# A quarter of the tokens sent ahead through every stage with unsplit weights, and more tokens moved from dense experts to gathered rows

## The chip, the core and the metric

The program runs on one core of one Trainium2 chip. The metric is the device time of one execution in microseconds (us). The engines are TensorE (PE, matmuls), VectorE (DVE), ScalarE (ACT), GpSimd (POOL) and the queues that issue transfers (SP's above all).

## What is computed

The reference is one residual block on x of 512 tokens by 2048 channels, all in float32:

```python
h  = rms_norm(x)
q, k, v, forget, pool_in, gates = split(h @ W_in)       # 8 heads x 128; pool 1024; two gates x 2048
yA = forgetting_attention(q, k, v, log_sigmoid(forget)) # causal, logits + sum of log f
yB = multiscale_pool(pool_in)                           # trailing means of 2, 4, 8, 16 tokens
x  = x + (sig(gA) * (yA @ W_A) + sig(gB) * (yB @ W_B)) @ W_out
xn = rms_norm(x)
# per token and head: 16 of 16384 experts by two lists of 128 keys (top 16 of each, then of their sums)
a   = u[idx] . xn                    # one number for each of 8 x 16 experts
x   = x + sum(gelu(a) * softmax_gate * v[idx])
```

An expert is one row of u and one row of v (2048 numbers each). The attention of a token needs the keys and values of all earlier tokens.

## The kernel before

**Weights as a stream.** Every weight tile is [128, 2048] float32, 1 MB. `plan` lists the tiles in the order of use; `ensure_load` (L112, the transfer is L116) brings them on SP's queue into `wraw` (three buffers). `ensure_split` makes two parts that TensorE takes at its fast rate: ScalarE casts `whi` (L131), then VectorE, for 28 tiles GpSimd, subtracts `wlo` (L133); two buffers each. `next_w` hands out tile n and has tile n+1 split at that place of the program. Activations are split in the same manner. `mm3` (L165 to L167) is three matmuls for each pair of blocks: high by high, high by low, low by high. A tile is 16 blocks, 48 matmuls.

**Stages.** All 512 tokens go together as columns through 64 tiles of input projections (with pooling, and attention head by head), 16 of the branch projection (`wbr`), 16 of the output projection (`wo`) and 16 of the query (`wqu`), with the top-k lists. Then the experts: the first 384 tokens are dense. For them all 16384 experts are computed: 128 tiles `uT` (128 experts each) give `a`, gelu, times a gate matrix that is zero except at the chosen experts, and 128 tiles `vd` bring the result back to channels. The first 64 u tiles run before any v tile and their results are spilled to `a_d`; meanwhile the gate matrix is built from comparisons (`o`, L801, L802, L804), small full-precision matmuls (L789) and copies to `stg`, and stored in `g_d`. Then come 192 tiles of u and v in turn.

**Gathered rows.** For the last 128 tokens the chosen rows are gathered: 128 indirect transfers of u (128 tokens x 2048, L832), each followed on VectorE by a multiply with a sum (L817), then 128 of v with a multiply and add (L823). Two buffers `row`; they are spread evenly over the 256 expert tiles.

**Who sets the order.** Each engine takes its instructions in the order of the program. Between two weight tiles the program calls `run_gens`, which lets every Python generator in `gens` (attention, norms, top-k, gates, the products `h_make` with the gates) issue its next piece. In an expert tile of before the rows come after that:

```python
        hi, lo = next_w()      # cast whi, subtract wlo of the next tile
        run_gens()
        rows_use()
        ps = acc_bank()
        mm3(ps[:, :ND], wterms(hi, lo, xnh, xnl))
```

`h_make` (L886) multiplies a block `at` (or a spilled one, `sp`) with its gates on VectorE, casts it on ScalarE (`h5h`) and subtracts on VectorE (`h5l`). A tick below is the work between two weight tiles.

Of the kernel before, what the change touches and what calls it, by code (L numbers as in the profile page):

```python
# [29 lines left out]
ND = 384  # L30
NDB = ND // P
# [8 lines left out]
LEAD = 14  # L40
QS = 2


@with_exitstack
def block_kernel(ctx, tc, a):
# [5 lines left out]
    wsp = ctx.enter_context(tc.tile_pool(name="wsp", bufs=2))  # L51
    psm = ctx.enter_context(tc.tile_pool(name="psm", bufs=4, space=bass.MemoryType.PSUM))
    psx = ctx.enter_context(tc.tile_pool(name="psx", bufs=4, space=bass.MemoryType.PSUM))
# [10 lines left out]
    z_d = dram.tile([2 * KD, P, S], F32, name="z_d")  # L64
    ap_d = dram.tile([4, P, 4, S], F32, name="ap_d")
    x2_d = dram.tile([4, P, 4, S], F32, name="x2_d")
    x2t_d = dram.tile([P, D], F32, name="x2t_d")
    a_d = dram.tile([LAG, P, IG, ND], F32, name="a_d")
    c_d = dram.tile([H, S], F32, name="c_d")
    g_d = dram.tile([NC, P, P, TC], F32, name="g_d")  # L70

    # weight stream: every tile is [128, 2048], read once, split into two float32r parts
    plan = []

    def flat(ap):
        return ap.rearrange("p j t -> p (j t)")

    order1 = [("g", 0), ("g", 1), ("pin", 0), ("pin", 1), ("pg", 0)] + [("pin", i) for i in range(2, 8)]
    gi = 2
    for h in range(H):  # L80
        order1 += [("q", h), ("k", h), ("v", h)] + [("g", gi + i) for i in range(3)]
        gi += 3
    order1 += [("g", i) for i in range(gi, 2 * KD)]
    src1 = dict(g="wgl", pin="wpin", q="wq", k="wk", v="wv")
    for kind, i in order1:
        plan.append((a["wpg"] if kind == "pg" else a[src1[kind]][i],
                     None if kind == "pg" else "dve"))
    for i in range(KD):
        plan.append((a["wbr"][i], "dve"))
        if i == 0:  # L90
            for c in (2, 3, 0):
                plan.append((flat(ap_d[c]), None))
    for i in range(KD):
        plan.append((a["wo"][i], "dve"))
    for i in range(KD):
        plan.append((a["wqu"][i], "pool"))
    seq = [("u", g) for g in range(LAG)]
    for g in range(LAG, NIG):
        seq += [("u", g), ("v", g)]
        if g - LAG < LAG:  # L100
            seq.append(("v", g - LAG))
    for n, (kind, g) in enumerate(seq):
        for i in range(4):
            eng = "pool" if n < 3 else "dve"
            if kind == "u":
                plan.append((a["uT"][g * IG + i], eng))
            else:
                plan.append((a["vd"][4 * g + i], eng))
# [11 lines left out]
    def ensure_split(n):  # L120
        while st["split"] <= min(n, len(plan) - 1):
            i = st["split"]
            st["split"] += 1
            eng = plan[i][1]
            if eng is None:
                n += 1
                continue
            ensure_load(i)
            raw = raws.pop(i)
            hi = wsp.tile([P, D], F32R, name="whi")  # L130
            nc.scalar.copy(hi, raw)  # L131
            lo = wsp.tile([P, D], F32R, name="wlo")
            (nc.gpsimd if eng == "pool" else nc.vector).tensor_tensor(  # L133
                lo, raw, hi.bitcast(F32), op=OP.subtract)
            parts[i] = (hi, lo)

    def next_w(ahead=1):
        n = st["use"]
        st["use"] += 1
        ensure_split(n)  # L140
        if ahead:
            ensure_load(n + 2)
            ensure_split(n + ahead)
        return parts.pop(n)

    def next_raw():
        n = st["use"]
        st["use"] += 1
        ensure_load(n)
        st["split"] = max(st["split"], n + 1)  # L150
        return raws.pop(n).rearrange("p (j t) -> p j t", j=4)
# [20 lines left out]

    def split(pool, src, shape, tag, **kw):
# [11 lines left out]

    g1 = const.tile([P, KD], F32, name="g1")
    nc.scalar.dma_start(g1, a["g1"])

    # stage 1: input projections, pooling branch, forgetting attention
    es_h, ph = lpool("ph")  # L190
    hh = ph.tile([P, KD, S], F32R, name="hh")
    hl = ph.tile([P, KD, S], F32R, name="hl")
    es_0, p0 = rpool("p0")
    xr = []
    ensure_load(0)
    for c in range(4):
        t = p0.tile([P, 4, S], F32, name="x%d" % c)
        nc.sync.dma_start(t.rearrange("p j t -> p (j t)"), a["xT"][c])
        xr.append(t)
    ensure_load(2)  # L200
    ensure_split(0)

    for c in range(4):
        for j in range(4):
            k = 4 * c + j
            nc.scalar.activation(hh[:, k, :], xr[c][:, j, :], AF.Copy, scale=g1[:, k:k + 1])  # L206
            nc.vector.scalar_tensor_tensor(hl[:, k, :], xr[c][:, j, :], g1[:, k:k + 1],  # L207
                                           hh[:, k, :].bitcast(F32), op0=OP.mult, op1=OP.subtract)
    ensure_split(1)
    first_z = [acc_bank()]  # L210
    hi, lo = next_w(0)
    mm3(first_z[0], wterms(hi, lo, hh, hl))
    ensure_load(2)
    jp = p0.tile([P, P], I32, name="jp")
# [9 lines left out]
    nc.vector.memset(epsc, EPS)  # L224
    rcnt = const.tile([P, 16], F32, name="rcnt")
# [3 lines left out]
    nc.scalar.dma_start(g2, a["g2"])  # L229
    psc = const.tile([P, 8], F32, name="psc")  # L230
    nc.scalar.dma_start(psc, a["psc"])
    qg = const.tile([P, 1], F32, name="qg")
    nc.scalar.dma_start(qg, a["qg"])
    nc.vector.tensor_scalar(qg, qg, float(np.float32(P ** -0.5)), None, op0=OP.mult)
    kg = const.tile([P, 1], F32, name="kg")
    nc.scalar.dma_start(kg, a["kg"])
    fb = const.tile([H, 1], F32, name="fb")
    nc.scalar.dma_start(fb, a["fb"])

    ssqx = const.tile([P, S + NTB], F32, name="ssq")  # L240
    ssq = ssqx[:, :S]
    sqs = []
    for c in range(4):
        t = p0.tile([P, 4, S], F32, name="s%d" % c, bufs=1) if c < 2 else xr[c]
        nc.scalar.activation(t, xr[c], AF.Square)
        sqs.append(t)
        if c == 1:
            nc.vector.tensor_tensor(sqs[0], sqs[0], sqs[1], op=OP.add)
    hi, lo = next_w()
    nc.vector.tensor_tensor(sqs[2], sqs[2], sqs[3], op=OP.add)  # L250
    nc.vector.tensor_tensor(sqs[0], sqs[0], sqs[2], op=OP.add)
    nc.vector.tensor_tensor(sqs[0][:, 0:2], sqs[0][:, 0:2], sqs[0][:, 2:4], op=OP.add)
    nc.vector.tensor_tensor(ssq, sqs[0][:, 0], sqs[0][:, 1], op=OP.add)
    es_0.close()
    first_z.append(acc_bank())
    mm3(first_z[1], wterms(hi, lo, hh, hl))
    es_1, p1 = rpool("p1")
    rstd = p1.tile([P, S], F32, name="rstd")
    jq = p1.tile([P, P], I32, name="jq")
    nc.gpsimd.iota(jq, pattern=[[1, P]], base=0, channel_multiplier=-1)  # L260
    onesr = p1.tile([P, P], F32R, name="onesr")
    nc.vector.tensor_copy(onesr, ones)
    mask = p1.tile([P, P], F32, name="mask")
    nc.vector.tensor_scalar(mask, jq, 0.0, 1.0e30, op0=OP.is_gt, op1=OP.mult)

    def rsqrt_of(out, tmp, ms, dst=None):
        nc.scalar.activation(out, ms, AF.Ln, bias=epsc[:, 0:1], scale=1.0)
        nc.scalar.activation(out, out, AF.Exp, scale=-0.5)
        nc.vector.tensor_tensor(tmp, out, out, op=OP.mult)
        nc.vector.scalar_tensor_tensor(tmp, ms, epsc[:, 0:1], tmp, op0=OP.add, op1=OP.mult)  # L270
        nc.vector.tensor_scalar(tmp, tmp, -0.5, 1.5, op0=OP.mult, op1=OP.add)
        nc.vector.tensor_tensor(out if dst is None else dst, out, tmp, op=OP.mult)

    def mean_bcast(sq, n, ms):
        ps = bank()
        nc.tensor.matmul(ps, lhsT=ones, rhs=sq, start=True, stop=True)
        nc.scalar.activation(ms, ps, AF.Copy, scale=1.0 / n)

    def input_norm():
        mean_bcast(ssq, D, ssq)  # L280
        t = p1.tile([P, S], F32, name="sc", bufs=4)
        rsqrt_of(rstd, t, ssq)

    def scaled(ps, tag, bufs):
        t = p1.tile([P, S], F32, name=tag, bufs=bufs)
        nc.vector.tensor_tensor(t, ps, rstd, op=OP.mult)
        return t

    def gate(i, ps):
        z = scaled(ps, "zg", 2)  # L290
        if i == 2 * KD - 1:
            nc.sync.dma_start(z_d[i], z)
        else:
            gens.append(gate_out(i, z))

    def gate_out(i, z):
        nc.sync.dma_start(z_d[i], z)
        yield

    mixes = {}  # L300

    def pool_in(i, ps):
        g, kc = divmod(i, 2)
        w = WINDOWS[g]
        raw = scaled(ps, "qkv", 3)
        cur, step = raw, 1
        while step < w:
            nxt = p1.tile([P, S], F32, name="sc", bufs=4)
# [9 lines left out]
        if kc == 1:  # L318
            gens.append(pool_group(g))
# [125 lines left out]
    for n, (kind, i) in enumerate(order1):  # L445
        if n < 2:
            continue
# [588 lines left out]
```

## Time and profile before

| | us |
|---|---|
| median of 3 runs | 3636.14 (3634.03 to 3636.44) |
| span of the profiled execution | 3634.7 |
| TensorE busy | 3555.3 |
| VectorE busy | 2435.5 |
| ScalarE busy | 1383.7 |
| GpSimd busy | 458.9 |
| projections with attention, about | 9 to 794 |
| branch, output, query stages, about | 794 to 1343 |
| first 64 u tiles and gate matrix, about | 1343 to 2066 |
| u and v tiles, about | 2066 to 3631 |

The profiled execution's span is 1.4 us under the median, so the sums below are made against the span and carried over with that difference. A busy share is an average over stages with different limits; the stages are read from windows.

### The profile page before, as it was taken

The numbers are of one execution on the slowest core, as the hardware profiler recorded it, in microseconds if no ns is written. First come the engines' busy times: TensorE is split into PE (matmuls) and PEld (weight loads), VectorE is DVE, ScalarE is ACT, GpSimd is POOL, SyncE is SP. The second block draws the span as 40 slices with busy tenths as digits, with TensorE's granted clock in tenths as the row PEclk, the third lists the DMA queues.
The fourth block names the chain that finished last, engine by engine and source line by source line (L and its number), as shares of the span: only waits on it lengthen the run. The fifth ranks groups of instructions, "written<-read, shape, count | busy, mean of one in ns | idle before, by whom it ended". The sixth has DMA issues, their size and how long they took to land.

```text
span 3634.7 us, 46381 instructions
## 1 busy us (share of the span) xinstructions
PE 3555.3 (98%) x19033; PEld 3315.7 (91%) x19033; DVE 2435.5 (67%) x3348; ACT 1383.7 (38%) x1735; POOL 458.9 (13%) x330
## 2 busy tenths in 40 slices
PE   8999999999999997699999999999999999999999
PEld 6788888878888877699999999999999999999999
DVE  5555445534432899466666677888888877778886
ACT  4343334323322431488887322222222222222222
POOL 0000000000001653111101111111111111111110
PEclk9999999999999998799999999999999999999999
DMA  4223332244444332378888978888788888788885
GB/s 186 87 103 109 110 113 99 102 169 146 154 145 137 116 113 100 120 284 300 279 281 291 342 279 293 292 288 292 277 302 281 289 290 282 272 288 293 288 291 203
DMA packets 187124, 789.56 MB, mean 217 GB/s; under 512 B 16264, under 2 KB 86920, under 8 KB 103840
## 3 DMA queue, kind: packets, MB, share of 16 engines
q1 hardware_dynamic: 132992, 469.80, 37.5%
q0 software_dynamic: 37040, 269.57, 20.6%
q10 hardware_dynamic: 16880, 47.23, 3.6%
q8 instruction: 149, 2.44, 0.3%
q14 instruction: 63, 0.52, 0.0%
HBM read 726.75 MB, written 59.79 MB: 216 GB/s over the span
## 4 chain that ended last, share of the span: by engine, by line
PE 92%; DVE 5%; issue 2%; POOL 1%; ACT 0%; DMA 0%; SPq 0%; POOLq 0%; ACTq 0%
PE psm L167 24%; PE psm L165 24%; PE psm L166 24%; PE psx L167 5%; PE psx L166 5%; PE psx L165 5%; PE psx L789 2%; DVE cf L675 1%; POOL wlo L133 0%; DVE pi L692 0%; DVE eqm L695 0%; DVE ix L622 0%; DVE s L617 0%; DVE ix L615 0%; DVE sel L703 0%
## 5 line engine op out<-in xcount | busy, mean ns | idle before, releaser
L133 DVE TENSOR_TENSOR wlo<-wraw,whi 128x2048 fp32r<-128x2048 f32 x340 | 781.7, 2299 | 533.3 <-ACT whi L131 533.1
L131 ACT CAST whi<-wraw 128x2048 fp32r<-128x2048 f32 x368 | 702.8, 1910 | 686.9 <-PE psm L166 360.6
L165 PE MATMUL psm<-xnh,whi 128*128 128x384 f32 x2048 | 696.4, 340 | 44.7 <-ACT whi L131 44.7
L167 PE MATMUL psm<-xnh,wlo 128*128 128x384 f32 x2048 | 692.0, 338 | 11.9 <-POOL wlo L133 11.9
L166 PE MATMUL psm<-xnl,whi 128*128 128x384 f32 x2048 | 691.5, 338 | 0.0
L165 PEld LDWEIGHTS psm<-xnh,whi 128*128 128x128 f32 x2048 | 387.8, 189 | 45.7 <-ACT whi L131 45.5
L165 PE MATMUL psm<-hh,whi 128*128 128x512 f32 x1024 | 403.8, 394 | 11.9 <-ACT hh L206 9.3
L167 PE MATMUL psm<-hh,wlo 128*128 128x512 f32 x1024 | 401.6, 392 | 1.3 <-DVE wlo L133 1.3
L166 PE MATMUL psm<-hl,whi 128*128 128x512 f32 x1024 | 401.0, 392 | 0.6 <-DVE hl L207 0.6
L167 PEld LDWEIGHTS psm<-xnh,wlo 128*128 128x128 f32 x2048 | 387.4, 189 | 13.2 <-POOL wlo L133 13.2
L166 PEld LDWEIGHTS psm<-xnl,whi 128*128 128x128 f32 x2048 | 387.8, 189 | 0.0
L167 PE MATMUL psx<-h5h,wlo 128*128 128x384 f32 x1024 | 342.3, 334 | 0.0
L165 PE MATMUL psx<-h5h,whi 128*128 128x384 f32 x1024 | 342.3, 334 | 0.0
L166 PE MATMUL psx<-h5l,whi 128*128 128x384 f32 x1024 | 342.2, 334 | 0.0
L167 PE MATMUL psm<-h5h,wlo 128*128 128x384 f32 x1024 | 342.1, 334 | 0.0
L166 PE MATMUL psm<-h5l,whi 128*128 128x384 f32 x1024 | 342.1, 334 | 0.0
L165 PE MATMUL psm<-h5h,whi 128*128 128x384 f32 x1024 | 342.1, 334 | 0.0
L823 DVE SCALAR_TENSOR_TENSOR tok<-row,gact,tok 128x2048 f32<-128x2048 f32 x128 | 300.3, 2346 | 2.8 <-DMA row<-v,gidx 2.6
L817 DVE SCALAR_TENSOR_TENSOR row<-row,tok 128x2048 f32<-128x2048 f32 x128 | 292.1, 2285 | 0.1
L832 POOL DMA_INDIRECT row<-u,gidx x128 | 136.3, 1065 | 960.0 <-DVE row L817 949.9
L832 POOL DMA_INDIRECT row<-v,gidx x128 | 137.5, 1074 | 845.8 <-DVE tok L823 800.7
L165 PEld LDWEIGHTS psm<-hh,whi 128*128 128x128 f32 x1024 | 193.6, 189 | 52.3 <-ACT hh L206 9.3
(263 smaller groups left out, 5392.0 us busy)
## 6 DMA issues: line engine op xcount, KB each, us to landing
wraw<-uT SPq DMA_DIRECT2D x128, 1024.0 KB, 5.3
wraw<-vd SPq DMA_DIRECT2D x128, 1024.0 KB, 4.9
wraw<-wgl SPq DMA_DIRECT2D x32, 1024.0 KB, 5.0
g_d<-stg ACTq DMA_DIRECT2D x12, 2048.0 KB, 8.9
gt<-g_d SPq DMA_DIRECT2D x32, 768.0 KB, 7.6
wraw<-wbr SPq DMA_DIRECT2D x16, 1024.0 KB, 7.7
wraw<-wo SPq DMA_DIRECT2D x16, 1024.0 KB, 4.9
wraw<-wqu SPq DMA_DIRECT2D x16, 1024.0 KB, 5.1
```

The source lines that it names most:

```text
L131: nc.scalar.copy(hi, raw)
L133: (nc.gpsimd if eng == "pool" else nc.vector).tensor_tensor(lo, raw, hi.bitcast(F32), op=OP.subtract)
L165: nc.tensor.matmul(ps, lhsT=wh, rhs=xh, start=first and i == 0, stop=False)
L166: nc.tensor.matmul(ps, lhsT=wh, rhs=xl, start=False, stop=False)
L167: nc.tensor.matmul(ps, lhsT=wl, rhs=xh, start=False, stop=last and i == n - 1)
L675: nc.vector.tensor_tensor(cf.rearrange("p (a b) -> p a b", a=TK), prev[0][:, :, None].to_broadcast([P, TK, TK]), prev[1][:, None, :].to_br ...
L789: nc.tensor.matmul(pg[:, j * P:(j + 1) * P], lhsT=o1[:, j, :], rhs=o2[:, j, :], start=True, stop=True)
L817: nc.vector.scalar_tensor_tensor(r, r, 1.0, tok, op0=OP.mult, op1=OP.mult, accum_out=gact[:, j:j + 1])
L823: nc.vector.scalar_tensor_tensor(tok, r, gact[:, j:j + 1], tok, op0=OP.mult, op1=OP.add)
L832: nc.gpsimd.indirect_dma_start(out=r, out_offset=None, in_=a["u"] if n < HK else a["v"], in_offset=bass.IndirectOffsetOnAxis(ap=gidx[:, j: ...
```

## The change

The first 128 tokens (`NA`) go alone through projections, attention, branch, output, query and top-k, with the weight tiles as they are: `mm1` takes them unsplit in full precision, 16 matmuls of 128 columns a tile. Their 112 weight tiles are loaded for them a first time. Then the other 384 tokens (`NB`) go through the same stages as before, with split weights loaded again; keys and values of the first 128 are kept in DRAM. Under these stages the 256 rows of the first 128 tokens are gathered, from the projections on, at a rate of rows a tile that `RATE_B1`, `RATE_B2` and `RATE_LAG` set. Of the 384 tokens the last 64 (`NG`) are gathered too, two lists' halves to a slot (`GQ`), 128 more rows, so 384 rows in all, and 320 (`ND`) are dense. All `wlo` are on VectorE. The top-k of two of the three later token blocks moves from the query stage into the first 64 u tiles, beside the gate matrix. v tiles are cut differently (8 experts' blocks by 256 channels, eight tiles a group of one u group and one spilled group), and `rows` is called ahead of `run_gens`.

```diff
-ND = 384
-NDB = ND // P
+NA = P
+NB = S - NA
+NBB = NB // P
+ND = 320
+NG = NB - ND
+GQ = P // NG
...
+RATE_B1 = 1.5
+RATE_B2 = 1.35
+RATE_LAG = 0.75
...
+    for order, eng in ((order_a, None), (order_b, "dve")):
+        for kind, i in order:
+            plan.append((a[src1[kind]][i], eng))
+        for name in ("wbr", "wo", "wqu"):
+            for i in range(KD):
+                plan.append((a[name][i], eng))
...
+        seq += [("u", g), ("v", g - LAG)]
+    for kind, g in seq:
+        if kind == "u":
+            plan += [(a["uT"][g * IG + i], "dve") for i in range(IG)]
+        else:
+            plan += [(a["vd"][8 * g + i], "dve") for i in range(8)]
...
-            (nc.gpsimd if eng == "pool" else nc.vector).tensor_tensor(
-                lo, raw, hi.bitcast(F32), op=OP.subtract)
+            nc.vector.tensor_tensor(lo, raw, hi.bitcast(F32), op=OP.subtract)
...
+    def mm1(ps, raw, x, k0=0, n=KD, m=P):
+        for k in range(n):
+            nc.tensor.matmul(ps, lhsT=raw[:, (k0 + k) * m:(k0 + k + 1) * m], rhs=x[:, k0 + k, :],
+                             start=k == 0, stop=k == n - 1)
...
+    def rows(rate):
+        if not row["on"]:
+            return
+        row["credit"] = min(row["credit"] + rate, 3.0)
+        while row["credit"] >= 1.0 and row["n"] < len(items) and items[row["n"]][0] == row["grp"] \
+                and row["grp"] < row["ready"]:
+            if len(row["live"]) == 2:
+                if row["hold"]:
+                    return
+                row_use()
+            if len(row["live"]) < 2:
+                row_load()
+            row["credit"] -= 1.0
...
+    def u_tile(at, rate):
         hi, lo = next_w()
+        rows(rate)
         run_gens()
-        rows_use()
         ps = acc_bank()
         mm3(ps[:, :ND], wterms(hi, lo, xnh, xnl))
         nc.scalar.activation(at, ps[:, :ND], AF.Gelu_apprx_tanh)
...
+    def h_make(at, gt, i):
+        av = at.rearrange("p (c t) -> p c t", t=TC)
+        nc.vector.tensor_tensor(av, av, gt[:, :, i, :], op=OP.mult)
+        hp = (p6.tile([P, ND], F32R, name="h5h", bufs=2 * IG), p6.tile([P, ND], F32R, name="h5l", bufs=2 * IG))
+        nc.scalar.copy(hp[0], at)
+        nc.vector.tensor_tensor(hp[1], at, hp[0].bitcast(F32), op=OP.subtract)
+        return hp
+
+    def h_later(hps, n, at, gt, i):
+    left_rows = len(items) - row["n"]
+    ticks = 12 * (NIG - LAG)
+    rate = left_rows / (ticks - 8)
...
+    for g in range(LAG):
+        hps = {}
+        for i in range(IG):
+            at = p7.tile([P, ND], F32, name="at", bufs=3)
+            gens.append(h_later(hps, IG + i, sps.pop((g, i)), gts, i))
+            if i + 2 < IG:
+                spilled(g, i + 2)
+            u_tile(at, rate)
+            if i < IG - 1:
+                gens.append(h_later(hps, i, at, gtu, i))
             else:
+                hps[i] = h_make(at, gtu, i)
+        if g + 1 < LAG:
+            gtu, gts = g_in(LAG + g + 1), g_in(g + 1)
+            spilled(g + 1, 0)
+            spilled(g + 1, 1)
+        order = [IG, IG + 1, IG + 2, IG + 3, 0, 1, 2, 3]
+        for s in range(8):
+            hi, lo = next_w()
+            rows(rate)
             run_gens()
+            ps = psv.tile([P, 2, S], F32, name="psv")
+            for j in range(2):
+                mm3(ps[:, j, :ND], [(hi[:, e * 256 + j * P:e * 256 + (j + 1) * P],
+                                     lo[:, e * 256 + j * P:e * 256 + (j + 1) * P],
+                                     hps[e][0], hps[e][1]) for e in order])
+            ac = acc[:, 2 * s:2 * s + 2, :]
+            nc.vector.tensor_tensor(ac, ac, ps[:, :, :ND], op=OP.add)
```

On VectorE in the projections, at the end of an attention head: last score block, softmax, and the transposed weights `PL` (TensorE's transposes wait for the softmax). Before, reciprocals and scaling were in one piece with the scores:

```order
L410 SCALAR_TENSOR_TENSOR pr<-ck,cT,psx 128x512
L412 TENSOR_TENSOR pr<-pr,mask 128x128
L413 TENSOR_REDUCE sm<-pr 128x1
L419 RECIPROCAL sm<-sm 128x1
L420 TENSOR_SCALAR pr<-pr,sm 128x128
...
L420 TENSOR_SCALAR pr<-pr,sm 128x512
L286 TENSOR_TENSOR zg<-psm,rstd 128x512
L133 TENSOR_TENSOR wlo<-wraw,whi 128x2048
L432 TENSOR_TENSOR PL<-psx,PH 128x512
```

Of the change:

```order
L868 SCALAR_TENSOR_TENSOR pr<-ck,cT,psx 128x512
L870 TENSOR_TENSOR pr<-pr,mask 128x128
L871 TENSOR_REDUCE sm<-pr 128x1
L139 TENSOR_TENSOR wlo<-wraw,whi 128x2048
L679 SCALAR_TENSOR_TENSOR row,gact<-row,tok 128x2048 x2
L878 RECIPROCAL sm<-sm 128x1 x3
L139 TENSOR_TENSOR wlo<-wraw,whi 128x2048
L679 SCALAR_TENSOR_TENSOR row,gact<-row,tok 128x2048
L892 TENSOR_TENSOR PHL<-psx,PHL 128x384 x2
```

The reciprocals have moved one tick behind the scores, and a subtract and two rows stand ahead of them; the scaling is on ScalarE now (L879), and the transposes (L889) stand on TensorE ahead of the tile of the tick after that.

On VectorE in the first 64 u tiles, a tick of before, with the comparisons `o` for the gate matmuls of the tick after:

```order
L133 TENSOR_TENSOR wlo<-wraw,whi 128x2048
L802 TENSOR_SCALAR o_10591<-iot,i2T,gT 128x128 x4
L802 TENSOR_SCALAR o_10602<-iot,i2T,gT 128x128 x4
L817 SCALAR_TENSOR_TENSOR row,gact<-row,tok 128x2048 x2
L133 TENSOR_TENSOR wlo<-wraw,whi 128x2048
```

Of the change, a tick with one head of the top-k (its first rows and its last):

```order
L139 TENSOR_TENSOR wlo<-wraw,whi 128x2048
L682 SCALAR_TENSOR_TENSOR tok<-row,gact,tok 128x2048
L562 MAX v_12533<-sl 128x8
L562 MAX v_12534<-sl 128x8
...
L569 MAX tops<-cf 128x8
L571 MAX_INDEX pos<-tops,cf 128x8
L1221 TENSOR_SCALAR o_12567<-iot,id_11748,id_11749 128x128 x4
L1221 TENSOR_SCALAR o_12578<-iot,id_11748,id_11749 128x128 x4
L139 TENSOR_TENSOR wlo<-wraw,whi 128x2048
```

A row and the whole head of the top-k stand between the subtract and the comparisons now; every second tick has such a head.

On VectorE in a u tick of the last 192 tiles, before:

```order
L133 TENSOR_TENSOR wlo<-wraw,whi 128x2048
L887 TENSOR_TENSOR at<-at,gt 128x384
L891 TENSOR_TENSOR h5l<-at,h5h 128x384
L823 SCALAR_TENSOR_TENSOR tok<-row,gact,tok 128x2048
L133 TENSOR_TENSOR wlo<-wraw,whi 128x2048
```

Of the change:

```order
L139 TENSOR_TENSOR wlo<-wraw,whi 128x2048
L682 SCALAR_TENSOR_TENSOR tok<-row,gact,tok 128x2048
L1276 TENSOR_TENSOR at<-at,gt 128x320
L1279 TENSOR_TENSOR h5l<-at,h5h 128x320
L1276 TENSOR_TENSOR sp<-sp,gt 128x320
L1279 TENSOR_TENSOR h5l<-sp,h5h 128x320
L139 TENSOR_TENSOR wlo<-wraw,whi 128x2048
```

The row has moved ahead of the products with the gates, and a tick makes two of them, the spilled block's too.

## Rows read from the trace of the kernel before

**Rows 1.** The page: busy time of the engines, and the chain that ended last

```profile
PE 3555.3 (98%) x19033; PEld 3315.7 (91%) x19033; DVE 2435.5 (67%) x3348; ACT 1383.7 (38%) x1735; POOL 458.9 (13%) x330
...
PE 92%; DVE 5%; issue 2%; POOL 1%; ACT 0%; DMA 0%; SPq 0%; POOLq 0%; ACTq 0%
```

**Rows 2.** Windows: length; busy (instructions) by engine; PEclk, DMA share, GB/s

```profile
150.00:650.00 500.00, 500.00 (x2292) 415.95 (x2291) 254.78 (x359) 201.27 (x253) 0.00 (x0) 1.00 0.30 105
1990.00:2066.00 76.00, 76.00 (x443) 76.00 (x442) 43.56 (x33) 24.52 (x23) 7.49 (x8) 1.00 0.96 347
2066.00:2850.00 784.00, 784.00 (x4523) 783.78 (x4522) 626.36 (x650) 224.89 (x189) 113.95 (x104) 1.00 0.82 289
```

**Rows 3.** Timeline of PE, projections: start, length

```profile
299.65 0.39 PE L167 MATMUL psm<-hh,wlo 128*128 128x512 f32 x1
...
301.01 0.39 PE L167 MATMUL psm<-hh,wlo 128*128 128x512 f32 x1
```

**Rows 4.** Timeline of PE, a u tile

```profile
1345.04 0.34 PE L167 MATMUL psm<-xnh,wlo 128*128 128x384 f32 x1
...
1348.16 0.34 PE L167 MATMUL psm<-xnh,wlo 128*128 128x384 f32 x1
```

**Rows 5.** Chain that ended last, in order of time, gate matmuls

```profile
1513.51 1.78 PE psx L789 x16
```

**Rows 6.** The page: costliest groups, xcount | busy, mean ns | idle before

```profile
L133 DVE TENSOR_TENSOR wlo<-wraw,whi 128x2048 fp32r<-128x2048 f32 x340 | 781.7, 2299 | 533.3 <-ACT whi L131 533.1
L131 ACT CAST whi<-wraw 128x2048 fp32r<-128x2048 f32 x368 | 702.8, 1910 | 686.9 <-PE psm L166 360.6
...
L817 DVE SCALAR_TENSOR_TENSOR row<-row,tok 128x2048 f32<-128x2048 f32 x128 | 292.1, 2285 | 0.1
```

**Rows 7.** The page: DMA issues, KB each, us to landing

```profile
wraw<-uT SPq DMA_DIRECT2D x128, 1024.0 KB, 5.3
...
g_d<-stg ACTq DMA_DIRECT2D x12, 2048.0 KB, 8.9
...
wraw<-wbr SPq DMA_DIRECT2D x16, 1024.0 KB, 7.7
```

**Rows 8.** Window of VectorE in the top-k: three lists

```profile
1423.38:1427.60 4.22, 4.19 (x25) 1.00 0.80 266
```

**Rows 9.** Groups of VectorE, 150 to 650 us, widest score block

```profile
L410 DVE SCALAR_TENSOR_TENSOR pr<-ck,cT,psx 128x512 f32<-128x512 f32 x7 | 5.2, 737 | 0.0
...
L413 DVE TENSOR_REDUCE sm<-pr 128x1 f32<-128x512 f32 x7 | 4.8, 686 | 0.2
```

**Rows 10.** Groups of ScalarE, 150 to 650 us, widest exponential

```profile
L414 ACT ACTIVATE pr<-pr,sm 128x512 f32<-128x512 f32 x7 | 5.1, 724 | 6.9 <-DVE sm L413 6.9
```

**Rows 11.** Timeline of VectorE, first 64 u tiles

```profile
1607.51 2.29 DVE L133 TENSOR_TENSOR wlo<-wraw,whi 128x2048 fp32r<-128x2048 f32 x1 [3.56 <-ACT whi L131]
1609.72 2.14 DVE L802 TENSOR_SCALAR o<-iot,i2T,gT 128x128 f32<-128x128 f32 x8
1611.78 2.28 DVE L817 SCALAR_TENSOR_TENSOR row<-row,tok 128x2048 f32<-128x2048 f32 x1
```

**Rows 12.** Timeline of ScalarE, first 64 u tiles

```profile
1604.63 0.49 ACT L861 ACTIVATE as<-psm 128x384 f32<-128x384 f32 x1 [1.53 <-PE psm L167]
...
1605.57 1.91 ACT L131 CAST whi<-wraw 128x2048 fp32r<-128x2048 f32 x1 [0.45 <-ACT as L861]
```

**Rows 13.** Timeline of VectorE, v tiles

```profile
2478.95 0.55 DVE L887 TENSOR_TENSOR sp<-sp,gt 128x384 f32<-128x384 f32 x1
2480.08 0.56 DVE L891 TENSOR_TENSOR h5l<-sp,h5h 128x384 fp32r<-128x384 f32 x1 [0.58 <-ACT h5h L890]
```

**Rows 14.** Timeline of PE after a stop

```profile
1360.10 0.69 PE L167 MATMUL psm<-xnh,wlo 128*128 128x384 f32 x1 [4.02 <-POOL wlo L133]
...
1361.86 0.53 PE L166 MATMUL psm<-xnl,whi 128*128 128x384 f32 x1
...
1364.10 0.49 PE L167 MATMUL psm<-xnh,wlo 128*128 128x384 f32 x1
```

More of the change, by code (lines that the diff above doesn't have):

```diff
@@ L274, in mean_bcast @@
[L274 to L292, printed above, removed]
-        else:
-            gens.append(gate_out(i, z))
@@ new lines, in narrow_rstd, with row_bcast @@
+    def narrow_rstd(b, n):
+        v = ssn[:, b:b + n]
+        nc.vector.tensor_scalar(v, v, 1.0 / D, EPS, op0=OP.mult, op1=OP.add)
+        rsqrt_nr(rsn[:, b:b + n], v, tmn[:, b:b + n])
+    def row_bcast(pool, cols, name):
+        ps = bank()
+        n = len(cols)
+        for j, c in enumerate(cols):
+            dg = pool.tile([P, P], F32, name="dg", bufs=2)
+            nc.vector.tensor_scalar(dg, ident, c, None, op0=OP.mult)
+            nc.tensor.matmul(ps[:, j * P:(j + 1) * P], lhsT=ones, rhs=dg, start=True, stop=True)
+        out = pool.tile([P, n * P], F32, name=name)
+        nc.scalar.copy(out, ps[:, :n * P])
+        return out
@@ L392, in attend @@
-    def attend(h, v):
+        nc.tensor.matmul(ps[:, :n], lhsT=ones, rhs=sq, start=True, stop=True)
+        v = pool.tile([P, n], F32, name=tags, bufs=bufs)
+        nc.scalar.activation(v, ps[:, :n], AF.Identity, bias=epsc[:, 0:1], scale=1.0 / P)
+        r = pool.tile([P, n], F32, name=tags, bufs=bufs)
+        t = pool.tile([P, n], F32, name=tags, bufs=bufs)
+        rsqrt_nr(r, v, t)
+        nc.vector.scalar_tensor_tensor(out, raw, gain[:, 0:1], r, op0=OP.mult, op1=OP.mult)
+    qkA = {}
@@ new lines, in attendA @@
+        vA = p1.tile([P, 4, P], F32, name="vA")
+        nc.scalar.copy(vA.rearrange("p j t -> p (j t)"), pv)
+        nc.scalar.dma_start(vA_d[hb], vA)
+        ck = p1.tile([P, 4, NA], F32, name="ck")
+        for j in range(4):
+            h = 4 * hb + j
+            nc.sync.dma_start(ck[:, j, :], c_d[h:h + 1, :NA].to_broadcast([P, NA]))
+        yield
+        yield
+        qn, kn = qkA.pop((0, hb)), qkA.pop((1, hb))
+        pss = bank()
+        for j in range(4):
+            nc.tensor.matmul(pss[:, j * P:(j + 1) * P], lhsT=qn[:, j, :], rhs=kn[:, j, :],
+                             start=True, stop=True)
@@ new lines, in block_kernel, with start_rows @@
+    for i in range(KD):
+        raw = next_raw()
+        if i == KD - 1:
+            ensure_load(st["use"] + 2)
+        run_gens()
+        j = i % 4
+        if j == 0:
+            ps = acc_bank()
+        mm1(ps[:, j * P:(j + 1) * P], raw, nA)
+        if j == 3:
+            gens.append(scores_a(i // 4, ps))
+    ensure_split(st["use"])
+    while gens:
+        run_gens()
+    def start_rows():
+        yield from tok_u(x2t_d, rstA[:, 0:1])
+        for _ in blkA.decode():
+            yield
+        blkA.index(gidx[0])
+        row["on"] = True
+        row["ready"] = 1
+        yield
+        yield from blkA.softmax()
+        nc.vector.tensor_copy(ggat[0], blkA.tops)
+        es_k.close()
@@ L653, in norm_gen @@
-        assert done[1] == KD
+        load(0)
+        load(1)
+        for k in range(KD):
+            part(k)
+            if k + 2 < KD:
+                load(k + 2)
+            if k > 0:
+                yield
+    blk3 = Block(pt_)
     def retrieve(h, q2, kk):
         yield
-        ss = []
+        s3 = [pt_.tile([P, P], F32, name="s%d" % half, bufs=2) for half in range(2)]
+        sd = p4.tile([P, 2, NB - P], F32, name="sd", bufs=2)
         for half in range(2):
             pss = bank()
-            for b in range(NTB):
+            for b in range(NBB):
```

1436 lines of the change are left out of this document (825 added, 611 removed).

## The prediction, made before the changed kernel had run

> **What bounds the kernel now.** I read the page first: TensorE is busy for 98% of the span and is 92% of the chain that ended last [rows 1]. So the time is its matmuls plus the gaps between them, and the reader should see that there are few gaps: in the 500 us window of the input projections TensorE is busy throughout while VectorE has 254.8 us of work, and in the expert stage it is busy throughout again while VectorE has 626.4 of 784 [rows 2]. Then the timeline, for the pace at which matmuls are issued: 512 columns, six steps in 1.36 us, 0.227 us each [rows 3]; 384 columns, 18 steps in 3.12 us, 0.1735 each [rows 4]. The line through the two gives an estimate of 0.1468 for 320 columns. A weight tile is 48 such matmuls: 10.9, 8.33 and 7.04 us. A full-precision matmul of 128 columns is two records, and 8 of them take 1.78 us, 0.224 each [rows 5].
>
> By stages the old kernel is: 64 + 16 + 16 + 16 tiles of 512 columns, 1221 us; 256 tiles of 384 columns, 2132; 384 gate matmuls, 86; attention products, small matmuls and the two ends, some 84. That is 3523, and 112 of the profiled span of 3634.7 are gaps or matmuls at half pace. The median shown, 3636.1, is 1.4 above the span.
>
> **What the change takes from TensorE and gives to it.** The 112 projection tiles drop from 512 to 384 columns: 112 x (10.9 - 8.33) = 288 us less. The 256 expert tiles drop from 384 to 320: 256 x (8.33 - 7.04) = 330 less. Gate matmuls for 64 tokens fewer: 14 less. Added is the stage of the first 128 tokens: 112 tiles x 16 full-precision matmuls x 0.224 = 401, and about 22 for its attention and transposes. Attention loses a query block, some 5. With the small matmuls of the rebuilt stages (about +18) the work without gaps is about 3326, 197 less than before. What decides is the gaps: if they come to under 309 us, the kernel gets faster.
>
> **What it adds to VectorE.** 128 more gathered rows at 2.3 us [rows 6], 295 us; the subtract of 28 tiles that GpSimd did, 64; and a full row pass now stands in every stage from the second on: 86 rows in the 64 projection tiles, 65 in the branch, output and query stages, 49 in the 64 first expert tiles, 184 in the last 192 (counted in the order of rows). VectorE then has 50 to 60% (projections) and 80% (experts) of TensorE's time, so on the average nothing binds. But the rows now stand directly behind the subtract `wlo` and in front of everything that the generators issue. A row cannot be passed on VectorE, and whoever waits for the work behind it is late by it.
>
> **The gaps, stage by stage.** I walked each stage's rows in order, with the durations of before scaled to the new columns.
>
> First stage: 445 us. 401 + 22, 10 for the first loads, 12 for dependent short chains. A tile lasts 3.58 us, three buffers leave two tile times, 7.2 us, for a load that lands in 5.3 [rows 7]: covered; if loads took the 7.7 us of the branch's weights [rows 7], a tile would last 3.85, 30 us more in all. The rate is 1 MB (1.05e6 bytes) in 3.58 us, 293 GB/s, against 347 seen at a share of 0.96 [rows 2].
>
> Between the stages: 16 us. The top-k and its decode for the first 128 tokens stand on VectorE ahead of the first subtract; three lists cost 4.19 us [rows 8], so a head (two lists, the sum, one wide list) is some 5.45.
>
> Projections: 64 x 8.33 = 533, 19 for the pooling and forget products, 8 x 5.8 for attention, and gaps of 80. The place is the transposes L889 at the head of every sixth tile, which wait for the softmax. From the start of the tick with the scores: cast 1.9, subtract 2.2, row 2.4, three score blocks 4.0 (1.7 with its mask for the widest, less for the others), last exponential 0.7 and its read-out [rows 6, 9, 10], gives 11.4; the copy of the gate logits and the next cast, queued behind it on ScalarE, end at 14.2, the subtract at 16.4, two rows at 21.0, reciprocals and scalings at 22.9. TensorE comes to the transposes at two tiles and the score products, 18.3. That is 4.6 of waiting, 5 with what is carried over; the key norm, held by its two rows, costs 3.2, the transposes of v 0.9. Per head 9, eight heads 72, and the rest at the start. Together 678.
>
> Branch, output, query: 48 x 8.33 = 400, 15 for small matmuls, and gaps of 69: 18 at the start, where four chunks go through one buffer one after another instead of being loaded ahead; 15 in the branch (row ahead of the gate products: a cycle of 9.4 against 8.33, partly absorbed), 11 and 25 in the next two. Together 484.
>
> First 64 expert tiles: 64 x 7.04 = 450, gate matmuls 72, gaps 90. Before, `wlo` and the comparisons `o` were alone ahead of the gate matmuls: VectorE waits 3.56 us for the cast, then 2.2 and 2.1 [rows 11]. Now a tick has subtract 2.2, row 2.4, a top-k head 5.45 and comparisons 2.1, 12.2 together. The cast begins when the last tile's gelu is read (0.9 after its end [rows 12]) and takes 1.9, so the comparisons end some 15 us after that tile's end; TensorE is back at the gate matmuls after 8.8, and waits about 6, less 0.7 carried over. Ten such pairs of ticks with a row, two without: 60. The start costs 8; at the end the gates are ready only with the last tile, a store of 8.9 us [rows 7] and the loads behind it leave 22. Together 612.
>
> Last 192 expert tiles: 192 x 7.04 = 1350 and 16 groups x 6. In a u tick ScalarE's casts `h5h` now wait for products that stand behind subtract and row, and the next weight cast stands behind them: 1.9 + 2.2 + 2.3 + two products, two casts, hand-offs of 0.58 [rows 13] and gelu, 9.3 against TensorE's 7.04. Four such ticks bring the chain some 9 behind; one tile of lead takes 3, and 2.0 + 4.0 appears at the first v tile, where the subtract and the last h are late. The v ticks (2.2 + 2.3 + 0.8) make it good again. Together 1446.
>
> The end, selection and output of the second gathered tokens: 8, before 4.
>
> Sum: 445 + 16 + 678 + 484 + 612 + 1446 + 8 = 3689, and 1.4 to the median: **3690 us**, 54 slower. The gaps in it are 363; the sum changes sign at 309.
>
> A 4.02 us stop in the old trace was followed by 384-column matmuls 0.32 apart instead of 0.1735, for 4 us at least [rows 14]: about 2 us lost. My gaps are mostly at or under 6 us; I take nothing for it. If each of some 16 long ones cost 2, it is 30 more; that is the upper bound I keep.
>
> The Trainium skill speaks against the first stage: TensorE: Matmul & The Clock Gate, section "HAM oscillation — how this bites in real kernels", tells of matmuls with M of 128 whose weight waits let the clock fall at every tile. By it the first stage would run at 1.2 GHz and its 401 us would double; by the row, where full-precision 128-column matmuls run at full pace between others, they stay 401. No run here shows a long stretch of them alone yet.
>
> **The rivals.** (a) *The gaps are covered* (0.27): VectorE is free for 20% or more, so the ticks could run ahead of TensorE and the rows fall into slack, above all in the head chain and the gate ticks. In the old trace the same engines never stopped TensorE in 784 us with rows of the same length [rows 2]. Against it: there the row stood behind the h work. With half of my gaps, 182, it is 3326 + 182 + 1 = 3510; it decides from 309 on. (b) *Loads bind* (0.10): the first stage at 4.4 us a tile (a landing of 8.8 us) is 90 more, 3780. For it: loads of 7.7 us happened [rows 7]. In the last stage the need is about 319 GB/s with gathers, gates and spilled activations, under 347. (c) *TensorE at half clock through the first stage* (0.03): at the slow pace of the old trace, 0.32 for 0.1735 [rows 14], its 401 us become 740, and the time about 4030. It needs a stop at nearly every tile, and loads of 5.3 us in 7.2 leave none. The Trainium skill's section named above describes this course.
>
> **How the numbers follow.** My sum has 0.60. Its own range is 3620 to 3760: gaps a fifth smaller, or 30 for the clock and 30 for late loads more. With (a) down to 3500, below which three quarters of my gaps would have to vanish or halve again, and up to 3780, about 2 in 10 stay outside. Faster by over 0.2% (some 7 us, what a measurement of this kernel can tell from no change): (a) and a small part of mine, 0.31; within it 0.06; slower 0.63.
>
> **What would show it.** In the new trace: the first stage ends near 445 with matmuls 0.112 apart; the list of waits names for TensorE L889 <- ScalarE's scaling, the gate matmuls <- VectorE's comparisons, and h or `wlo` at each group's first v tile; the expert stage has a period of 90 us per group, 84.4 if nothing waits. I am wrong if these waits are short, or if the first stage's clock falls.

## The result

The changed kernel takes 3907.72 us (median of 4 runs, 3905.65 to 3913.95) against 3635.09 for the kernel before: ratio 1.0756, interval 1.074 to 1.0771. It is slower by 273 us. The direction was forecast, the size was not: 3690 was predicted, and the range ended at 3780.

The page of the changed kernel, its busy time and its clock in 40 slices, answers to [rows 1]:

```profile
PE 3508.9 (90%) x22581; PEld 3425.3 (88%) x22581; DVE 2507.8 (64%) x3130; ACT 1362.5 (35%) x1779; POOL 455.8 (12%) x401
...
PEclk9999998999999999999999998999899999999998
```

Span 3904.9 less 3508.9 busy is 396 us in which TensorE stands still; the prediction had 363. But TensorE is also busy for 3508.9 us with work that was counted at 3326. That is 183 us too long, and the mean granted clock of this execution is 0.951. Windows of the five stages (length; busy and instructions of PE, PEld, DVE, ACT, POOL; PEclk, DMA share, GB/s), to be held against [rows 2]:

```profile
0.00:471.20 471.20, 432.83 (x3761) 426.43 (x3762) 108.37 (x310) 77.27 (x136) 5.56 (x15) 0.99 0.82 287
471.20:1201.40 730.20, 649.76 (x3453) 619.20 (x3452) 488.07 (x577) 286.41 (x393) 135.16 (x90) 0.94 0.68 241
1201.40:1695.30 493.90, 445.64 (x2413) 428.94 (x2414) 359.94 (x462) 163.26 (x222) 87.50 (x64) 0.95 0.77 284
1695.30:2350.00 654.70, 571.19 (x3788) 564.35 (x3787) 485.01 (x956) 397.35 (x642) 51.10 (x49) 0.93 0.64 233
2350.00:3895.00 1545.00, 1405.78 (x9164) 1385.37 (x9162) 1066.23 (x828) 435.89 (x383) 176.47 (x183) 0.95 0.77 280
```

The reader should subtract the first number behind the comma from the length, and then compare it with the count of matmuls. In the projections (second row) TensorE idles 80 us, what was predicted to the microsecond, and is busy 650 for work counted at 598. The first stage, alone, has its clock (0.99) and its time.

Who made TensorE wait (engine, line, waited for: us in total, times, longest):

```profile
PE psm L172 <- DVE wlo L139: 65.1, 37, 6.1
PE psv L170 <- ACT h5h L1278: 63.3, 16, 13.5
PE psx L1205 <- DVE o L1221: 48.6, 12, 5.0
PE psv L172 <- DVE wlo L139: 41.1, 33, 1.8
PE psx L889 <- ACT pr L879: 37.2, 12, 5.5
PE psx L367 <- ACT sc L364: 25.7, 12, 2.7
```

All the waits that the prediction named are there. The timeline of TensorE at one of them, the transposes of a head in the projections, shows what follows a stop:

```profile
998.85 2.87 PE L889 MATMUL psx<-ident,pr 128*128 128x128 f32 x9 [4.27 <-ACT pr L879]
1001.37 0.67 PE L170 MATMUL psm<-hh,whi 128*128 128x384 f32 x1
1001.84 0.52 PE L171 MATMUL psm<-hl,whi 128*128 128x384 f32 x1
1002.16 0.52 PE L172 MATMUL psm<-hh,wlo 128*128 128x384 f32 x1
```

4.27 us of waiting, then matmuls 0.32 apart instead of 0.1735: the pace of [rows 14]. By the clock records of the two traces, TensorE is granted half its clock (1.2 GHz) in 6 stretches of the old kernel and in 72 of this one, 381.7 us in all. What was one of a few places follows stop after stop here.

The u tick of the last stage, VectorE and then ScalarE:

```profile
2865.42 2.29 DVE L139 TENSOR_TENSOR wlo<-wraw,whi 128x2048 fp32r<-128x2048 f32 x1 [1.63 <-ACT whi L137]
2867.63 2.28 DVE L679 SCALAR_TENSOR_TENSOR row<-row,tok 128x2048 f32<-128x2048 f32 x1
...
2869.84 0.48 DVE L1276 TENSOR_TENSOR at<-at,gt 128x320 f32<-128x320 f32 x1
...
2874.45 2.29 DVE L139 TENSOR_TENSOR wlo<-wraw,whi 128x2048 fp32r<-128x2048 f32 x1 [1.64 <-ACT whi L137]
```

```profile
2863.50 1.89 ACT L137 CAST whi<-wraw 128x2048 fp32r<-128x2048 f32 x1
2870.42 0.46 ACT L1278 CAST h5h<-at 128x320 fp32r<-128x320 f32 x1 [5.03 <-DVE at L1276]
2871.84 0.46 ACT L1278 CAST h5h<-sp 128x320 fp32r<-128x320 f32 x1 [0.96 <-DVE sp L1276]
2872.20 0.43 ACT L1248 ACTIVATE at<-psm 128x320 f32<-128x320 f32 x1
2872.53 1.89 ACT L137 CAST whi<-wraw 128x2048 fp32r<-128x2048 f32 x1
```

From one `whi` cast to the next it is 9.03 us (predicted 9.3) against 7.04 of matmuls. ScalarE stands 5.03 us behind the subtract and the row with the next weight tile ready to be cast. The Trainium skill, Perfetto Trace Analysis, section "Tensor Engine Instruction (MATMUL, LD_WEIGHTS)", says that the queues of ScalarE and VectorE are strictly first in, first out; this timeline agrees.

### The profile page after: what moved, and what is told of

It reads as the page before. It is cut to its first block, busy times and chain, and to the rows that moved or that the text cites. A ratio compares the mean times of both kernels' runs of the same rounds, so it can differ in the third digit from the quotient of the medians.

```text
span 3904.9 us, 53787 instructions
## 1 busy us (share of the span) xinstructions
PE 3508.9 (90%) x22581; PEld 3425.3 (88%) x22581; DVE 2507.8 (64%) x3130; ACT 1362.5 (35%) x1779; POOL 455.8 (12%) x401
## 5 line engine op out<-in xcount | busy, mean ns | idle before, releaser
L170 PE MATMUL psv<-h5h,whi 128*128 128x320 f32 x2048 | 653.0, 319 | 75.1 <-ACT h5h L1278 63.3
L172 PE MATMUL psv<-h5h,wlo 128*128 128x320 f32 x2048 | 652.1, 318 | 41.1 <-DVE wlo L139 41.1
L172 PE MATMUL psm<-xnh,wlo 128*128 128x320 f32 x2048 | 641.8, 313 | 28.8 <-DVE wlo L139 28.6
L170 PE MATMUL psm<-xnh,whi 128*128 128x320 f32 x2048 | 645.4, 315 | 17.6 <-ACT whi L137 17.6
L171 PE MATMUL psv<-h5l,whi 128*128 128x320 f32 x2048 | 651.4, 318 | 0.3
L171 PE MATMUL psm<-xnl,whi 128*128 128x320 f32 x2048 | 640.1, 313 | 0.0
L170 PEld LDWEIGHTS psv<-h5h,whi 128*128 128x128 f32 x2048 | 400.0, 195 | 81.0 <-ACT h5h L1278 67.5
L172 PEld LDWEIGHTS psv<-h5h,wlo 128*128 128x128 f32 x2048 | 399.1, 195 | 50.0 <-DVE wlo L139 50.0
L171 PEld LDWEIGHTS psv<-h5l,whi 128*128 128x128 f32 x2048 | 399.4, 195 | 4.2 <-DVE h5l L1279 4.2
L170 PE MATMUL psm<-hh,whi 128*128 128x384 f32 x1024 | 364.1, 356 | 0.0
```

The lines of the kernel that those rows point to most:

```text
L170: nc.tensor.matmul(ps, lhsT=wh, rhs=xh, start=first and i == 0, stop=False)
L171: nc.tensor.matmul(ps, lhsT=wh, rhs=xl, start=False, stop=False)
L172: nc.tensor.matmul(ps, lhsT=wl, rhs=xh, start=False, stop=last and i == n - 1)
```

## The experiments

Theory: the gathered rows, put ahead of other work on VectorE, stop TensorE at many places, and behind each stop TensorE runs slowly for some microseconds. Rivals: VectorE simply has too much to do; the DMA engines are full; the clock is low for a reason that has nothing to do with the stops. The kernel before measured 3631.53 to 3637.12 beside these runs. Most have one time each, and the four times of the fastest version lie 18 us apart, so differences under some 20 us between them say nothing.

**Rows behind the generators.** In all stages:

```diff
-        rows(rate)
         run_gens()
+        rows(rate)
```

> The only edit: in every tick the gathered rows are issued behind the pieces of the generators instead of ahead of them. If the order on VectorE makes the stops (my theory), the dense group falls from about 92 to 84 to 87 us, the waits at L889 shrink, and with the stops the TensorE time at half clock goes: 3600 to 3750 us in all. If it is the sheer amount of VectorE work (rival), the time stays above 3850.

Measured 3763.01, 145 less than the change as it was given, and 13 over the expected range; clock 0.968. Windows of the projections and of the last stage from its first v tile on (188 tiles), then the same last stage of the changed kernel:

```profile
477.10:1133.10 656.00, 621.56 (x3453) 596.69 (x3452) 490.91 (x578) 287.58 (x393) 172.80 (x91) 0.98 0.73 271
2264.70:3750.10 1485.40, 1375.29 (x9026) 1356.55 (x9024) 1041.64 (x806) 431.62 (x372) 222.46 (x179) 0.97 0.77 282
```

```profile
2392.30:3893.80 1501.50, 1382.79 (x9026) 1363.34 (x9024) 1050.92 (x809) 427.09 (x372) 173.62 (x180) 0.96 0.77 280
```

The projections fall from 730 to 656 with the same work on VectorE (491 us), idle time from 80 to 34 and the busy time by 28 with it. Order, not amount, did that. The last stage hardly moved: it was 1501.5 and is 1485.4. My expectation for it (84 to 87 us a group) failed; something else held it.

**No rows.**

```diff
-            items += [(grp, kind, j, HK // q) for j in range(HK // q)]
+            pass
```

> No row is gathered at all (the gathered tokens' experts are left out, all other work stays). My theory, stops come mostly from rows ahead of other work: dense group about 84.4 us, projections near 620, 3450 to 3560 in all, granted clock 0.98 or more. Rival, the stops come from late weight loads and chains without rows: above 3650.

This leaves out the experts of the gathered tokens. Measured 3543.66, clock 0.986. The windows:

```profile
473.90:1118.10 644.20, 618.36 (x3454) 596.46 (x3453) 293.49 (x401) 288.37 (x393) 0.00 (x0) 0.99 0.37 127
2190.50:3530.60 1340.10, 1327.53 (x9026) 1323.32 (x9024) 641.43 (x557) 433.56 (x370) 0.00 (x0) 1.00 0.49 170
```

So the rows cost 364 us of the changed kernel's 3907.7, more than the 273 by which it is slower. This also bounds what any order of the rows could reach with the rest as it is.

**Matmuls in the stops.** A helper issues n matmuls that nobody reads, ahead of the transposes, of the late gate matmuls and of each group's first v tile:

```diff
+    def warm(n, w, x):
+        ps = acc_bank()
+        for i in range(n):
+            nc.tensor.matmul(ps[:, :x.shape[-1]], lhsT=w, rhs=x, start=True, stop=True)
...
+        warm(24, hh[:, 0, :P], hh[:, 1, :])
```

> Matmuls whose result nobody reads are put on TensorE ahead of three kinds of stop (24 of 384 columns ahead of each head's transposes, 24 of 320 ahead of the gate matmuls behind a top-k head, 30 of 320 ahead of each group's first v tile); waits and order of all else stay. If the stops themselves let the clock fall (theory), the clock rises from 0.951 to 0.975 or more and the time falls by 60 to 120 us although TensorE has 150 us more to do: 3790 to 3850. If the clock falls for another reason (rival), it stays at 0.95 and the time is the same or up to 50 us longer.

Measured 3884.75, 23 less, clock 0.971: both short of what I expected. Not all stops were covered, and much of the added work was longer than the stop it filled: in the last stage, with 450 more matmuls, idle time falls from 119 to 77 us and the stage still grows by 8. The projections show the effect alone, for there the filling (8 x 24 x 0.1735 = 33 us) fits the stops:

```profile
473.60:1177.80 704.20, 660.60 (x3646) 633.31 (x3645) 488.10 (x577) 286.86 (x393) 136.89 (x90) 0.98 0.69 248
```

Idle time fell by 37 (80.4 to 43.6) and 33 us of matmuls were added, yet busy time grew by only 11: the other 22 us had been the slow pace. The clock records say the same: TensorE is busy at half the clock for 73 us of the projections without the filling and for 22 with it. The order on VectorE and its work are untouched. The clock follows the stops.

**Gates ahead of the top-k.**

```diff
-    gens.append(topk_gen())
     gens.append(gate_gen())
+    gens.append(topk_gen())
```

> The only edit: the gate generator is called ahead of the top-k generator, so the comparisons stand ahead of a top-k head on VectorE. Theory: the wait of the gate matmuls for the comparisons (48.6 us in 12 stops) goes to under 10, with 20 to 25 us of half clock beside it, 3830 to 3860 in all. Rival, the wait moves to the subtract behind the top-k head: the time stays within 20 us of 3907.

Measured 3866.69, 41 less, 7 above the expected range. The wait of the gate matmuls in the first 64 u tiles (and the subtract, where the rival saw it go):

```profile
PE psm L172 <- DVE wlo L139: 24.6, 12, 6.0
PE psx L1205 <- DVE o L1221: 13.1, 9, 2.5
```

48.6 became 13.1, the subtract's stayed at 24.6 (24.7 in the change). The wait was that of the queue order and did not move on.

**Loads of the next group later on SP.** The last stage still had stops. SP's timeline of the changed kernel at the end of a group's u tiles:

```profile
2889.90 1.79 SPq L1270 DMA_DIRECT2D gt<-g_d  x2
2891.79 3.41 SPq L1293 DMA_DIRECT2D sp<-a_d  x2
2895.30 16.37 SPq L124 DMA_DIRECT2D wraw<-vd  x5
```

The queue issues nothing from 2868 to 2889.9. The gates of the next group wait for their buffer until this one's last products are made, and the v weights stand behind them. The queue's own waits in the last stage have this as their second largest, 22 us a group:

```profile
SPq L1270 <- DVE sp L1276: 328.7, 15, 22.0
```

On ScalarE of the changed kernel the casts waited for these weights:

```profile
ACT whi L137 <- DMA wraw<-vd: 198.1, 31, 26.3
```

With the rows moved alone, this lateness reaches TensorE once in each of 15 groups, some two tiles behind the first v tile:

```profile
PE psv L170 <- ACT whi L137: 46.7, 15, 7.1
```

```diff
-        if g + 1 < LAG:
-            gtu, gts = g_in(LAG + g + 1), g_in(g + 1)
-            spilled(g + 1, 0)
-            spilled(g + 1, 1)
...
+            if s == 3 and g + 1 < LAG:
+                gtu, gts = g_in(LAG + g + 1), g_in(g + 1)
+            if s == 4 and g + 1 < LAG:
+                spilled(g + 1, 0)
+                spilled(g + 1, 1)
```

> Rows behind the generators, and in the last 192 tiles the loads of the next group's gates and spilled blocks are put on SP's queue in the middle of the v tiles instead of ahead of the first one. Theory: the casts that wait 219 us for late v weights stop waiting, because those weights stood on SP behind a gate load that waited for its buffer; the last stage falls from 1485 to 1400 to 1430 us, 3680 to 3710 in all. Rival (the DMA engines are simply full): the weights are as late as before and the time stays within 25 us of 3763.

Measured 3660.04, 103 less than the rows moved alone and 20 under the expected range. The last stage, and the same wait on ScalarE:

```profile
2263.80:3646.90 1383.10, 1340.68 (x9025) 1330.22 (x9024) 1042.95 (x805) 430.11 (x372) 225.76 (x179) 0.99 0.81 302
```

```profile
ACT whi L137 <- DMA wraw<-vd: 27.6, 3, 17.7
```

The DMA engines were not full: the same bytes now pass at 302 GB/s instead of 282, and the waits for v weights are gone but for 27.6 us.

**Row work without gathers.** The rows behind the generators, VectorE's row work on one buffer of zeros, no gather transfers; the gathered tokens' experts are left out:

```diff
-        r = row_tile()
-        nc.gpsimd.indirect_dma_start(out=r, out_offset=None, in_=a[kind],
-                                     in_offset=bass.IndirectOffsetOnAxis(ap=gidx[grp][:, j:j + 1],
-                                                                         axis=0))
+        r = fixed
```

> Rows behind the generators; VectorE does the same row work, but on one buffer of zeros and without the gather transfers (the gathered tokens' experts are left out). If VectorE's work is what is left of the rows' cost, the time stays near 3763, 3720 to 3770; if it is the traffic of the gathers, it falls to 3560 to 3640.

Measured 3625.93, at the upper part of what I expected of traffic. The last stage:

```profile
2228.40:3613.10 1384.70, 1342.59 (x9025) 1328.45 (x9024) 1040.49 (x805) 429.87 (x372) 0.00 (x0) 1.00 0.48 168
```

This does not make traffic the cause there: with the traffic, and the loads in another order (the run before), that stage is 1383 us, here 1385. Gathers and the blocked queue cost these 100 us only together; either repair alone took them away. Ahead of the last stage this run is 36 us quicker than the one with the rows moved alone (its first v tile starts at 2228.4 instead of 2264.7). Whether that is the traffic or the row work's waits for its rows was not separated.

**Combination, and its rate.** Rows behind the generators, loads later, gates first, two buffers instead of one at the start of the branch stage:

> Three repairs together on top of the rows behind the generators: loads late as in the run before, the gate generator ahead of the top-k generator, two buffers for the attention and pooling outputs at the start of the branch stage. Theory: 3625 to 3680, with a clock of 0.98. Rival: repairs overlap and it stays above 3700.

Measured 3625.93, just inside the expected range, clock 0.981. With `RATE_B1 = 1.9` on top:

> As the combination, with 1.9 rows a tile in the projections instead of 1.5, so some 26 rows fewer in the last stage. If the last stage's VectorE work is what costs there, 10 to 20 us less than the combination; if the projections have no slack for it, 10 to 40 more.

Measured 3716.56, 91 more: worse than either expectation. The projections, at 1.5 and then at 1.9 rows a tile:

```profile
479.40:1132.20 652.80, 619.89 (x3454) 595.16 (x3453) 491.01 (x579) 287.19 (x393) 174.41 (x91) 0.99 0.73 273
```

```profile
475.10:1235.20 760.10, 657.79 (x3453) 623.54 (x3452) 542.75 (x626) 286.43 (x393) 209.91 (x115) 0.94 0.72 267
```

VectorE does 52 us more, and the stage is 107 longer: 33 us of idle time became 102, and the clock went with it. The last stage gave back 4, too little to tell from no change.

**Two versions that beat the kernel before.** The weight tile ahead of the first gate loads, then also `RATE_B2 = 1.0`:

```diff
+    ensure_load(st["use"] + 2)
     gtu = g_in(LAG)
```

> The combination of three repairs, and the weight tile that the third expert tile of the last stage needs is put on SP's queue ahead of the first gate, spill and accumulator loads. Theory: the stop of 16.7 us ahead of that tile goes to under 5, so 8 to 14 us less than the combination's 3626: 3610 to 3620, faster than before by 0.3 to 0.7%. Rival: the first v tile waits for its h instead and nothing is won.

Measured 3613.31 against 3636.16, ratio 0.9942, interval 0.9924 to 0.996; 3610 to 3620 was expected. The longest stop of the changed kernel, ahead of the third expert tile of the last stage, is down to 3.4 us here. It was:

```profile
PE psm L170 <- ACT whi L137: 17.6, 1, 17.6
```

> As the run beside it, with 1.0 rows a tile in the branch, output and query stages instead of 1.35, some 17 rows more in the last stage. If the 1.7 us stops of these stages come from ticks with two rows, they go with some 15 to 25 us; the last stage has VectorE room for 17 rows more and loses under 10: 3595 to 3615. If it has no room, 3620 to 3650.

Measured 3596.1 (3585.41 to 3603.56), ratio 0.9886, interval 0.986 to 0.9912: the fastest here, and inside what was expected. Its page:

```profile
PE 3402.0 (95%) x22581; PEld 3343.1 (93%) x22581; DVE 2504.9 (70%) x3130; ACT 1366.5 (38%) x1778; POOL 600.7 (17%) x401
```

The span of that execution is 3595.7, so TensorE still idles 194 us, half of what it did, and is busy 107 us less for the same matmuls. At half the clock it is busy for 89 us; in the change as it was given it was 285.

**The price of a stop, in the kernel before.** Two runs with nothing of the change in them. A small matmul in the third v tile of each of the 32 v groups waits for four short ScalarE operations on the tile before; in the second run 24 matmuls stand ahead of it (the loop over 24 below, which the first run does not have):

```diff
+    def stop():
+        nc.scalar.copy(dl, last_ps[-1][:, :ND])
+        for i in range(3):
+            nc.scalar.activation(dl, dl, AF.Relu)
+        ps = acc_bank()
+        for i in range(24):
+            nc.tensor.matmul(ps[:, :ND], lhsT=xnh[:, 0, :P], rhs=xnh[:, 1, :], start=True, stop=True)
+        nc.tensor.matmul(ps[:, :P], lhsT=dl[:, :P], rhs=ident, start=True, stop=True)
```

> The kernel before, with one stop of TensorE of about 4 us put into each of its 32 v groups: a small matmul waits for a chain of four short ScalarE operations on the tile before. If a stop costs its own length alone, the last stage grows by the idle time that the trace then shows, some 130 us, and the clock there stays 1.00. If the half clock behind it costs more (theory), it grows by some 60 us beyond the idle time: 3800 to 3850 in all.

> The same wait in the same places, but 24 matmuls that nobody reads (4.2 us) stand ahead of the waiting one, so TensorE works while it would wait. Theory: the clock stays 1.00 and the time grows by the 24 matmuls alone, 32 x 4.2 = 133: 3765 to 3785, 40 to 70 us less than the run beside it. Rival: both are the same within 15 us.

Measured 3911.32 and 3849.89. Both are longer than I expected: in every second group the chain on ScalarE stood behind a cast `h5h` that waited some 3.6 us for VectorE, so half of the stops were 8 us. The difference between the two was expected at 40 to 70: it is 61 us less, with more work. The last stage of the kernel before, of the one with stops, and of the one with the stops filled (the first window ends with its last v tile, the other two likewise):

```profile
2066.00:3631.00 1565.00, 1564.79 (x9024) 1564.25 (x9022) 1243.55 (x1222) 445.57 (x374) 212.68 (x199) 1.00 0.81 283
```

```profile
2066.00:3906.00 1840.00, 1648.94 (x9077) 1638.18 (x9075) 1256.25 (x1219) 505.86 (x500) 209.77 (x198) 0.94 0.68 241
```

```profile
2066.00:3845.00 1779.00, 1720.36 (x9860) 1709.57 (x9858) 1258.17 (x1222) 507.46 (x502) 212.75 (x199) 1.00 0.70 250
```

With the stops filled the clock is 1.00, and busy time grows by 156: 133 for the added matmuls and 23 for the small ones with what surrounds them. With stops TensorE idles 191 us and is busy 84 longer, of which the same 23 are not the stops' doing. The other 61 over 32 stops are 1.9 us for each on the average, beyond its length. By the clock records TensorE is busy at half the clock for 0, 152 and 10 us of the three windows. The filled kernel still waits at these places, and its clock stays at 1.00 all the same:

```profile
PE psm L907 <- ACT dl L903: 35.2, 16, 2.2
PE psm L906 <- DVE acc L934: 22.6, 16, 1.5
```

One stop of the shorter kind in the run with stops, on TensorE:

```profile
2245.00 0.79 PE L905 MATMUL psm<-ident,dl 128*128 128x128 f32 x2 [3.86 <-ACT dl L903]
2245.45 0.67 PE L165 MATMUL psx<-h5h,whi 128*128 128x384 f32 x1
2245.91 0.52 PE L166 MATMUL psx<-h5l,whi 128*128 128x384 f32 x1
2246.23 0.52 PE L167 MATMUL psx<-h5h,wlo 128*128 128x384 f32 x1
```

## Why the prediction was wrong in size

**The matmul work was right.** Where nothing stops TensorE the predicted paces hold: the run without rows is busy for 1328 us in the window from the first v tile on, which holds 188 tiles, by the prediction's 7.04 us 1324. The first stage with the transition was 461 and is 471.

**The gaps were nearly right.** 363 predicted, 396 measured. The stages' own terms add up to 373, and their work to 3316 instead of 3326; the sum of 3689 is the same. By stages: 38 and 38 to the end of the transition, 80 and 80 in the projections, 69 and 48 in branch to query, 186 and 223 in the expert stages. The transposes, the key norm, the late comparisons and the first v tile of a group appear as walked, at 37, 20 (in the projections), 49 and 63 + 41 us. What I left out in the last stage is SP's queue: the gate load that waits for a buffer ahead of the v weights, and the first loads of gates ahead of a weight tile (the stop of 17.6 us). With the rows moved alone that stage fell by 16, with the loads moved too by another 102; what the loads alone would give was not tried.

**The step that failed** is the sentence on the clock: "My gaps are mostly at or under 6 us; I take nothing for it", with 30 us kept as the upper bound. It is the term that was mis-sized, at 0, where TensorE was busy for 183 us beyond the counted work. The clock records give its share: TensorE is busy for 285 us at half the clock, where matmuls come 0.32 instead of 0.1735 us apart (384 columns), so an estimate of 130 of the 183 is the clock. The other 50 or so are not traced row by row. The first matmul behind a stop is longer too (0.67 us, 0.47 to the next, in the timeline above), and the old kernel too is busy beyond its count (3555.3 [rows 1] against 3523), at half the clock for 27 us. These 32 stood among the old kernel's 112 of "gaps or matmuls at half pace"; on the new kernel's side nothing stood for the like. With the counted work and the measured gaps alone the time would have been about 3724 (an estimate, 3326 + 396 and the 2 to 3 us from span to median), inside the range. That the stops cause the slow pace is shown by filling them, in the changed kernel's projections and in the kernel before. The row was there [rows 14], with its 2 us a stop; the failure was to take only 16 long stops even for the upper bound, where the six rows of waits above alone count 122, most of them shorter.

**The rivals.** Covered gaps (a) did not come: the ticks did not run ahead. Loads that bind the first stage (b) did not come: it moved 287 GB/s, and TensorE waited 0.9 us for weights in it; loads did bind in the last stage, but by their place in a queue. Half clock in the first stage (c) did not come: its clock is 0.99. The rule of the Trainium skill that I weighed (TensorE: Matmul & The Clock Gate, "HAM oscillation — how this bites in real kernels") rests on a wait for weights at every tile. The 128-column stage had nearly none, and its clock stayed up. That a wait makes the next stretch slow is what the later stages show, at 384 and 320 columns.

## What to carry to other kernels

A stop of a busy TensorE costs more than its length: in the kernel before, stops of 3.86 to 8.1 us cost 1.9 us each beyond it, on the average. So count the stops that a change makes, and do not only sum their time: the long ones carry a price of their own. What shorter ones cost was not measured apart; 32 waits of 1.4 to 2.2 us in the filled kernel left the clock where it was. A long instruction that nobody waits for belongs behind the short ones that somebody waits for, on a compute engine and on a DMA queue alike: here a call moved behind another, and two kinds of loads moved into the v tiles, brought 3907.7 to 3660 without taking a single instruction away. And when one wait is removed, look again: with the rows moved, TensorE waited in the v tiles for late weights instead, and their queue had stood still at that place before, too.

## What was not expected of the hardware

The 32 stops of 3.86 to 8.1 us were each followed by half the clock in the kernel before with its added waits, and so was a stop of 3.23 us in the changed kernel:

```profile
485.19 0.64 PE L172 MATMUL psm<-hh,wlo 128*128 128x384 f32 x1 [3.23 <-DVE wlo L139]
485.62 0.53 PE L170 MATMUL psm<-hh,whi 128*128 128x384 f32 x1
485.94 0.53 PE L171 MATMUL psm<-hl,whi 128*128 128x384 f32 x1
```

Filling the former with matmuls that nobody reads gave 61 us back although it added 133 us of work to TensorE. In the changed kernel the filling, less well fitted, gave 23.
